# One decoder layer on one core: new addresses for the parts of the weights, and a new order of the products of a pair

## The chip, the cores and the metric

The kernel runs on one core of a Trainium2 chip. The metric is the time that the device takes for one execution, in microseconds (us); the table further down has the median of three runs. One further execution was taken with the hardware profiler, and all rows below are from it.

The engines go by short names: PE is the matmul engine (TensorE), PEld its loads of stationary operands, DVE the vector engine, ACT the scalar engine, POOL GpSimd, SP the queue that issues most transfers.

## The reference

One layer of a decoder, for 256 tokens and 16 learned meta tokens in front of them, width 2048, all in float32: half a SwiGLU feed-forward step of hidden width 5632 (FFN1), a mixer of two attentions, and a second half step (FFN2). Cut to what matters:

```python
h = h + 0.5 * swiglu(rmsnorm(h, ffn1_norm), ffn1_w_gate, ffn1_w_up, ffn1_w_down)
proj = rmsnorm(h, mix_norm) @ w_in      # q, k, v of 8 + 8 heads, 8 forget logits, two gates of 2048
o_fox = forgetting_attention(...)       # softmax with a decay from the forget gates
o_sb = stick_breaking_attention(...)
merged = sigmoid(g_fox) * (o_fox @ w_branch_fox) + sigmoid(g_sb) * (o_sb @ w_branch_sb)
h = h + merged @ w_out
h = h + 0.5 * swiglu(rmsnorm(h, ffn2_norm), ffn2_w_gate, ffn2_w_up, ffn2_w_down)
return h[:, 16:]
```

`swiglu(x, g, u, d)` is `(silu(x @ g) * (x @ u)) @ d`. Nearly all of the arithmetic is in products of an activation with a weight matrix.

## The kernel before

**Products in three terms.** The kernel multiplies float32 matrices in the faster type float32r, and wins the accuracy back by splitting: ACT copies a weight tile `raw` into `wh` in float32r, DVE writes the rest, `raw - wh`, into `wl` (function `split`, lines 163 to 165). Activations are split in the same way into a high and a low half. Of the four products of the halves three are made: high by high, high by low and low by high, all accumulated in one bank of PSUM.

**Blocks and units.** A `Block` is a column range of one weight matrix, 512 columns wide as a rule. It is worked in units of 1024 / columns k tiles (of 128 rows), so two k tiles: a *pair*. `load(u)` brings a unit of 512 KB into one of five `raw` buffers by one transfer on SP's queue, `split_unit(u)` makes `wh` and `wl` (three buffers each), and `products(u)` issues the matmuls. `ahead(u)` keeps loads six units ahead and splits two units ahead of the products. All units follow each other in one list through FFN1, the mixer and FFN2; the attention and the evacuations are dealt out between the output tiles by `tick()`.

**Which operand is stationary.** Each matmul on PE has a stationary operand of up to 128 x 128, loaded before it, and a moving operand that streams past it. There are these kinds of block:

- by feature, 272 columns (FFN1's blocks and the k and v blocks of both attentions): a 128-column slice of the weights is stationary, a half of an activation tile (256 tokens and 16 meta tokens) moves. Four output tiles a unit, six products each, 24 a unit;
- by token (the two gates, the two branches, FFN2): a 128-token slice of an activation half is stationary, a 512-column weight part moves. Two output tiles a unit, six products each, 12 a unit;
- wide (the q blocks and w_out): both activation halves move in one product of 512 columns by `wh`, and the high half in one of 256 by `wl`;
- the forget gate, `stacked`: one unit of eight k tiles of 128 columns, two products each.

**What sets the order.** The order on PE is that of the loop in `products` (line 930 on): for each output tile, for each of the two k tiles, the three terms. By feature they are `wh` by high, `wh` by low, `wl` by high (line 941). By token they are high by `wh`, high by `wl`, low by `wh` (line 934). In the first 25 us the ACT and DVE instructions stand in a hand-written order (`first_start`, `first_norm`, `first_products`), and the scheduler brings forward PE's products that are ready; there the first block's units wait for x, for the split and for the transposes.

**Addresses.** An activation tile is `[P, 2, 2, 272]` (k tile, half, tokens) in FFN1 and the mixer and `[P, 2, 2, 256]` in FFN2 and for the attentions' outputs, so its halves lie 1088 or 1024 bytes apart in each partition. A weight part is `[P, 2, 512]`: k tiles 2048 bytes apart, slices of 128 columns 512 bytes apart. The built program places the bases of all these tiles at equal remainders modulo 256.

## Time and profile before

| | |
|---|---|
| median of 3 runs | 2249.6 us (2248.21 to 2250.57) |
| the profiled execution | 2249.19 us, its span 2247.5 us |
| mean granted clock of PE | 0.999 |
| PE busy | 2240.8 us, 13930 matmuls |
| loads of stationary operands | 2039.6 us |
| DVE, ACT busy | 1265.4 us, 1024.6 us |
| transfers | 403 MB, 179 GB/s on average |
| FFN1 | up to about 817 us |
| mixer | up to about 1520 us |
| FFN2 | the rest |

A group of the page's fifth part, and of the view by lines, has the line, the engine, the operation, the tile written and the tiles read (an arrow between them), the shapes and the count; then the busy time, the mean of one instruction, the idle time of the engine just before them and what ended most of it. Matmuls overlap in their pipeline: one of 272 columns lasts 288 ns from its start to its end, while the next starts some 125 ns after it. So a duration is not what a product costs; the distance from start to start is. In names of tiles `v` is an activation, `acc` and `aux` are banks of PSUM.

### The profile page before, as it was taken

The page shows a single profiled execution, that of the slowest core. Times are in us where ns is not written, and L with a number is a line of the kernel's source. Part 1 is how long each engine was busy: PE and PEld are TensorE (multiplying, and loading weights), DVE is VectorE, ACT ScalarE, POOL GpSimd, SP SyncE. Part 2 cuts the span into 40 slices and gives each one's busy share as a digit, 9 for nine tenths or more (in the row PEclk, how much of TensorE's full clock was granted, in tenths as well). Part 3 has the DMA queues.
Part 4 walks back from the last instruction along what each step waited for, and adds up shares of the span by engine and source line. Part 5 has one row for each costly group of instructions (what it writes and reads, how often), then busy time and mean ns, then how long its engine had stood idle before and what let it go on. Part 6 is the DMA issues. An engine that isn't in the chain of part 4 may idle for free.

```text
span 2247.5 us, 34143 instructions
## 1 busy us (share of the span) xinstructions
PE 2240.8 (100%) x13930; PEld 2039.6 (91%) x13930; DVE 1265.4 (56%) x1596; ACT 1024.6 (46%) x1280; POOL 42.1 (2%) x112
## 2 busy tenths in 40 slices
PE   9999999999999999999999999999999999999999
PEld 9999999999999999988899988888888888888887
DVE  6555544455555555987556666675445544544554
ACT  6444433334444454655446564454444433444433
POOL 1000000000000001110000000000000000000000
PEclk9999999999999999999999999999999999999999
DMA  7666655566665566555655556566666666666664
GB/s 228 171 177 178 172 177 177 171 178 176 172 177 175 173 184 180 158 167 167 194 180 151 150 150 187 181 185 178 188 190 193 187 191 194 191 190 190 188 199 156
DMA packets 211325, 403.03 MB, mean 179 GB/s; under 512 B 12680, under 2 KB 17632, under 8 KB 211168
## 3 DMA queue, kind: packets, MB, share of 16 engines
q1 hardware_dynamic: 209088, 397.33, 59.1%
q8 instruction: 109, 1.79, 0.3%
q10 hardware_dynamic: 1472, 2.37, 0.3%
q0 software_dynamic: 608, 1.16, 0.2%
q14 instruction: 48, 0.39, 0.1%
HBM read 398.70 MB, written 2.11 MB: 178 GB/s over the span
## 4 chain that ended last, share of the span: by engine, by line
PE 99%; DMA 0%; SPq 0%; DVE 0%; issue 0%; DVEq 0%; ACT 0%
PE acc L944 96%; PE aux L701 1%; PE aux L572 1%; PE aux L412 1%; PE aux L672 0%; PE aux L560 0%; PE acc L914 0%; DMA v<-in_meta_tokens_dram 0%; PE aux L828 0%; PE aux L312 0%; PE aux L651 0%; PE aux L652 0%; PE aux L653 0%; PE aux L615 0%; PE aux L616 0%; PE aux L238 0%
## 5 line engine op out<-in xcount | busy, mean ns | idle before, releaser
L165 DVE TENSOR_TENSOR wl<-raw,wh 128x1024 fp32r<-128x1024 f32 (+1 forms) x753 | 921.4, 1224 | 857.3 <-ACT wh L164 855.8
L164 ACT ACTIVATE wh<-raw 128x1024 fp32r<-128x1024 f32 (+1 forms) x753 | 797.2, 1059 | 1096.2 <-PE acc L944 1029.7
L944 PE MATMUL acc<-v,wh 128*128 128x272 f32 (+1 forms) x5776 | 1172.9, 298 | 0.0
L944 PEld LDWEIGHTS acc<-v,wh 128*128 128x128 f32 x5776 | 923.6, 189 | 22.7
L944 PE MATMUL acc<-wh,v 128*128 128x512 f32 x2880 | 905.9, 391 | 0.0
L944 PE MATMUL acc<-v,wl 128*128 128x272 f32 (+1 forms) x3128 | 897.0, 287 | 0.0
L944 PEld LDWEIGHTS acc<-wh,v 128*128 128x128 f32 x2880 | 540.6, 188 | 111.7
L944 PEld LDWEIGHTS acc<-v,wl 128*128 128x128 f32 x3128 | 587.4, 188 | 0.4 <-DVE wl L165 0.2
L944 PE MATMUL acc<-wl,v 128*128 128x512 f32 x1440 | 561.3, 390 | 0.0
L944 PEld LDWEIGHTS acc<-wl,v 128*128 128x128 f32 x1440 | 270.5, 188 | 54.6
L164 ACT ACTIVATE v<-aux 128x512 fp32r<-128x512 f32 (+1 forms) x46 | 23.7, 516 | 19.2 <-PE aux L412 11.9
L165 DVE TENSOR_TENSOR v<-aux,v 128x512 fp32r<-128x512 f32 (+1 forms) x46 | 27.4, 595 | 4.3 <-ACT v L164 2.6
L440 DVE TENSOR_TENSOR sq<-acc,rbc 128x272 f32<-128x272 f32 x44 | 19.3, 438 | 18.5 <-PE acc L944 17.3
L431 DVE TENSOR_TENSOR v<-acc,rbc 128x272 f32<-128x272 f32 x44 | 18.0, 436 | 15.7 <-PE acc L944 15.7
L164 ACT ACTIVATE v<-sq 128x272 fp32r<-128x272 f32 x44 | 17.4, 419 | 19.5 <-DVE sq L441 19.5
L432 ACT ACTIVATE v<-v 128x272 f32<-128x272 f32 x44 | 17.5, 424 | 13.8 <-DVE v L431 13.8
L473 DVE SCALAR_TENSOR_TENSOR v<-acc,v 128x272 f32<-128x272 f32 x32 | 12.9, 435 | 12.6 <-PE acc L944 12.6
L441 DVE TENSOR_TENSOR sq<-sq,v 128x272 f32<-128x272 f32 x44 | 19.3, 438 | 0.8
L852 ACT ACTIVATE v<-acc,rtok 128x512 f32<-128x512 f32 x22 | 15.2, 690 | 9.9 <-PE acc L944 9.7
L412 PEld LDWEIGHTS aux<-ident,v 128*128 128x128 f32 x120 | 14.8, 140 | 3.7
L165 DVE TENSOR_TENSOR v<-sq,v 128x272 fp32r<-128x272 f32 x44 | 18.2, 434 | 0.0
L412 PE MATMUL aux<-ident,v 128*128 128x128 f32 x120 | 17.9, 272 | 0.0
(219 smaller groups left out, 725.7 us busy)
## 6 DMA issues: line engine op xcount, KB each, us to landing
raw<-in_ffn_w_up_dram SPq DMA_DIRECT2D x176, 512.0 KB, 3.7
raw<-in_ffn_w_down_dram SPq DMA_DIRECT2D x176, 512.0 KB, 3.9
raw<-in_ffn_w_gate_dram SPq DMA_DIRECT2D x175, 512.0 KB, 3.7
raw<-in_w_in_dram SPq DMA_DIRECT2D x162, 512.0 KB, 3.7
raw<-in_w_out_dram SPq DMA_DIRECT2D x32, 512.0 KB, 3.9
raw<-in_w_branch_fox_dram SPq DMA_DIRECT2D x16, 512.0 KB, 3.9
raw<-in_w_branch_sb_dram SPq DMA_DIRECT2D x16, 512.0 KB, 3.9
v<-in_x_dram SPq DMA_DIRECT2D x8, 256.0 KB, 7.8
```

The source lines that it names most:

```text
L164: act.activation(hi, src, AF.Copy)
L165: dve.tensor_tensor(lo, src, hi.bitcast(F32), op=ALU.subtract)
L412: pe.transpose(p[:, (2 * j + i) * P:(2 * j + i + 1) * P], u[:, i, c:c + P], ident[:])
L431: dve.tensor_tensor(s, ps[:, :n], norm_of().r[:, :n], op=ALU.mult)
L432: act.activation(s, s, AF.Silu)
L440: dve.tensor_tensor(u, ps[:, :n], norm_of().r[:, :n], op=ALU.mult)
L441: dve.tensor_tensor(u, u, s, op=ALU.mult)
L473: dve.scalar_tensor_tensor(r, ps[:, :NT], 0.5, r, op0=ALU.mult, op1=ALU.add)
L572: pe.matmul(po[:, :NR], a[:, ks], b[:, i * NR:(i + 1) * NR], start=n == 0, stop=n == 6)
L701: pe.matmul(o, a, b, start=start, stop=stop, skip_group_check=True)
L852: act.activation(u["t"][:, i, :], ps[:], AF.Silu, scale=norms["ffn2"].rtok[:, i:i + 1])
L944: pe.matmul(o, a, c, start=first and m == 0, stop=last and m == len(terms) - 1, skip_group_check=wide)
```

## The change

Four things change.

1. Each `wh` and `wl` tile becomes a flat one of 1088 columns, and a part is placed in it by kind of block (`place`, `part_tile`). By feature with 272 columns: the k tiles are 544 columns apart (2176 bytes, instead of 2048), and `wh` begins 16 columns (64 bytes) into its tile. For the gates, whose activations have 272 columns too (`spaced`): also 544 apart, `wh` begins 32 and `wl` 16 columns into the tile. For all other blocks parts stay dense and begin at the start.
2. The six products of a pair follow a table of (k tile, part of the weights: 0 high, 1 low, half of the activation: 0 high, 1 low): `FEATURE`, `TOKEN`, or `PLAIN` for the rest. The wide blocks and the forget gate keep their order. With these tables and places the next stationary operand lies, modulo 256, 64 bytes past the start of the moving one in the 272-column blocks, and 0 bytes past it in all blocks by token.
3. To make room in the memory of a partition (the two tags with three buffers each grow by 256 bytes a buffer), constants are merged: the identity and the ones are held once, in float32r, and read as float32 where needed; `gcol1` and `grow1` become slices of `gcol` and `grow`; one transfer of `ffn1_norm` is dropped. POOL writes the identity and the ones into a temporary tile, and DVE copies them at the start.
4. `first_products`, for the first unit, keeps its order, on the new addresses.

```diff
+PLAIN = ((0, 0, 0), (0, 0, 1), (0, 1, 0), (1, 0, 0), (1, 0, 1), (1, 1, 0))
+FEATURE = ((0, 1, 0), (0, 0, 0), (0, 0, 1), (1, 1, 0), (1, 0, 0), (1, 0, 1))
+TOKEN = ((0, 0, 1), (1, 1, 0), (1, 0, 1), (0, 0, 0), (1, 0, 0), (0, 1, 0))
+PART = 1024 + 64
...
+    plain = temp([P, 2, NT], F32, "F3")
+    make_identity(nc, plain[:, 0, :P])
+    nc.gpsimd.memset(plain[:, 1, :P], 1.0)
...
+    dve.tensor_copy(identr[:], plain[:, 0, :P])
+    dve.tensor_copy(onesr[:], plain[:, 1, :P])
...
+    def place(b):
+
+        if b.by_token:
+            return (TOKEN, (32, 16), 32) if b.spaced else (PLAIN, (0, 0), 0)
+        return (FEATURE, (16, 0), 32) if b.n == NT and not b.stacked else (PLAIN, (0, 0), 0)
+
+    def part_tile(u, low):
+        b, k0, n = units[u]
+        tag = ("wh", "wl")[low]
+        t = wp.tile([P, PART], F32R, tag=tag, name=name(tag))
+        order, at, free = place(b)
+        w = b.cols + free
+        return t[:, :n * w].rearrange("p (k c) -> p k c", k=n)[:, :, at[low]:at[low] + b.cols]
...
     def split_unit(u):
         b, k0, n = units[u]
-        wh = wp.tile([P, n, b.cols], F32R, tag="wh", name=name("wh"))
+        wh = part_tile(u, 0)
...
-                if b.by_token:
-                    xh, xl = x[:, 0, cs], x[:, 1, cs]
-                    terms = ((ps[:], xh, wh[:, i, :]), (ps[:], xh, wl[:, i, :]), (ps[:], xl, wh[:, i, :]))
...
+            elif b.by_token:
+                terms = [(ps[:], x[i][:, m, cs], w[l][:, i, :]) for i, l, m in place(b)[0]]
+            else:
+                terms = [(ps[:, :b.n], w[l][:, i, cs], x[i][:, m, :b.n]) for i, l, m in place(b)[0]]
+            for m, (o, a, c) in enumerate(terms):
+                pe.matmul(o, a, c, start=k0 == 0 and m == 0, stop=k0 + n == b.kts and m == len(terms) - 1,
+                          skip_group_check=wide)
```

How this moves the instructions on PE, at three places. The first is a unit in the middle of FFN1, before (a row is a line, the operation, the bank written, the tiles read, the shape; x2 stands for two equal ones in a row; the numbers behind the names tell tiles apart):

```order
L944 MATMUL acc_4246<-v_1907,wh_4306 128x272 x2
L944 MATMUL acc_4246<-v_1907,wl_4307 128x272
L944 MATMUL acc_4246<-v_1907,wh_4306 128x272 x2
L944 MATMUL acc_4246<-v_1907,wl_4307 128x272
L944 MATMUL acc_4247<-v_1907,wh_4306 128x272 x2
L944 MATMUL acc_4247<-v_1907,wl_4307 128x272
```

and a unit of the same kind after:

```order
L968 MATMUL acc_3874<-v_2964,wl_4085 128x272
L968 MATMUL acc_3874<-v_2964,wh_4084 128x272 x2
L968 MATMUL acc_3874<-v_2964,wl_4085 128x272
L968 MATMUL acc_3874<-v_2964,wh_4084 128x272 x2
L968 MATMUL acc_3875<-v_2964,wl_4085 128x272
L968 MATMUL acc_3875<-v_2964,wh_4084 128x272 x2
```

Of each three products of a k tile the one with `wl` stood third, and stands first now; the two with `wh` follow it, by the high and then the low half of the activation.

The second is the first output tile of a gate's unit, between products of the attention, before:

```order
L944 MATMUL acc_10779<-wh_10671,v_7861 128x512
L944 MATMUL acc_10779<-wl_10672,v_7861 128x512
L944 MATMUL acc_10779<-wh_10671,v_7861 128x512 x2
L944 MATMUL acc_10779<-wl_10672,v_7861 128x512
L944 MATMUL acc_10779<-wh_10671,v_7861 128x512
L615 MATMUL aux_10787<-kqh_10737,onesr 128x272
```

and after:

```order
L968 MATMUL acc_10775<-wh_10667,v_7857 128x512
L968 MATMUL acc_10775<-wl_10668,v_7857 128x512
L968 MATMUL acc_10775<-wh_10667,v_7857 128x512 x3
L968 MATMUL acc_10775<-wl_10668,v_7857 128x512
L627 MATMUL aux_10783<-kqh_10733,onesr 128x272
```

The three products with `wh` that stand next to each other belong to both k tiles now, and the six visit the k tiles in turn.

The third is the first unit of line 944 at the start (transposes of x ahead of it), before:

```order
L312 MATMUL aux_253<-ident,v_126 128x128 x2
L312 MATMUL aux_254<-ident,v_126 128x128 x2
L944 MATMUL acc_198<-v_220,wh_227 128x272 x2
L944 MATMUL acc_199<-v_220,wh_227 128x272 x2
L944 MATMUL acc_200<-v_220,wh_227 128x272 x2
L944 MATMUL acc_201<-v_220,wh_227 128x272 x2
L944 MATMUL acc_198<-v_220,wl_228 128x272
L944 MATMUL acc_198<-v_220,wh_227 128x272 x2
```

and after (line 968 is the same call as line 944 before, line 324 the transposes):

```order
L324 MATMUL aux_251<-identr,v_124 128x128 x2
L324 MATMUL aux_252<-identr,v_124 128x128 x2
L968 MATMUL acc_196<-v_218,wl_226 128x272
L968 MATMUL acc_196<-v_218,wh_225 128x272 x2
L968 MATMUL acc_196<-v_218,wl_226 128x272
L968 MATMUL acc_196<-v_218,wh_225 128x272 x2
L968 MATMUL acc_197<-v_218,wl_226 128x272
L968 MATMUL acc_197<-v_218,wh_225 128x272 x2
```

The scheduler had put all eight products with `wh` and the high or low half of the first k tile ahead of the first with `wl`; now a product with `wl` is the unit's first.

## Rows read from the trace of the kernel before

**Rows 1.** The page's header, its first part (busy time, share of the span and instructions of each engine) and PE's line of its second part (40 slices of the span).

```profile
span 2247.5 us, 34143 instructions
PE 2240.8 (100%) x13930; PEld 2039.6 (91%) x13930; DVE 1265.4 (56%) x1596; ACT 1024.6 (46%) x1280; POOL 42.1 (2%) x112
...
PE   9999999999999999999999999999999999999999
```

**Rows 2.** The page's fourth part: the chain that ended last, by engine.

```profile
PE 99%; DMA 0%; SPq 0%; DVE 0%; issue 0%; DVEq 0%; ACT 0%
```

**Rows 3.** The page's fifth part, groups of instructions (columns as told above): the splits, and the loads of `wl`.

```profile
L165 DVE TENSOR_TENSOR wl<-raw,wh 128x1024 fp32r<-128x1024 f32 (+1 forms) x753 | 921.4, 1224 | 857.3 <-ACT wh L164 855.8
L164 ACT ACTIVATE wh<-raw 128x1024 fp32r<-128x1024 f32 (+1 forms) x753 | 797.2, 1059 | 1096.2 <-PE acc L944 1029.7
...
L944 PEld LDWEIGHTS acc<-v,wl 128*128 128x128 f32 x3128 | 587.4, 188 | 0.4 <-DVE wl L165 0.2
```

**Rows 4.** The view by lines on PE over the whole span, shapes kept apart: line 944.

```profile
L944 PE MATMUL acc<-v,wh 128*128 128x272 f32 x5264 | 991.4, 288 | 0.0
L944 PE MATMUL acc<-wh,v 128*128 128x512 f32 x2880 | 905.9, 391 | 0.0
L944 PE MATMUL acc<-v,wl 128*128 128x272 f32 x2616 | 753.4, 289 | 0.0
L944 PE MATMUL acc<-wl,v 128*128 128x512 f32 x1440 | 561.3, 390 | 0.0
```

**Rows 5.** Windows (us from the span's start; the length, then the busy time and count of each engine, then PE's granted clock as a share of 2.4 GHz, the share of the DMA engines and GB/s): two at the start, and one of FFN1.

```profile
7.40:10.80 3.40, 3.08 (x15) 2.94 (x14) 3.23 (x9) 1.11 (x3) 0.76 (x4) 0.50 1.01 342
...
14.20:20.00 5.80, 5.80 (x47) 5.59 (x46) 5.18 (x14) 5.80 (x23) 0.00 (x0) 1.00 1.07 354
300.00:600.00 300.00, 300.00 (x2391) 300.00 (x2391) 149.23 (x176) 115.39 (x128) 0.00 (x0) 1.00 0.58 175
```

**Rows 6.** Line 944 in a stretch of FFN1, 300 to 400 us: the form and count, the shortest, median and longest duration in ns, the start of the first and the last in us.

```profile
L944 PE MATMUL acc<-v,wh x532: 285/288/292, 299.9 to 399.9; 128*128 128x272 f32 x178
L944 PE MATMUL acc<-v,wl x266: 287/288/290, 299.8 to 399.6; 128*128 128x272 f32 x133
```

**Rows 7.** The same view in a stretch of FFN2, 1800 to 1900 us.

```profile
L944 PE MATMUL acc<-wh,v x295: 389/389/389, 1799.9 to 1899.9; 128*128 128x512 f32 x148
L944 PE MATMUL acc<-wl,v x148: 389/389/389, 1799.7 to 1899.6; 128*128 128x512 f32 x148
```

**Rows 8.** The same view in two instants of FFN1 (400.42 and 400.79 us), so that only two or three products are in it: the two of `wh` on the first k tile, then the two of `wh` on the second, and the two of `wl`.

```profile
L944 PE MATMUL acc<-v,wh x2: 289/290/292, 400.1 to 400.3; 128*128 128x272 f32 x2
L944 PE MATMUL acc<-v,wl x1: 287/287/287, 400.4 to 400.4; 128*128 128x272 f32 x1
...
L944 PE MATMUL acc<-v,wh x2: 285/286/287, 400.5 to 400.6; 128*128 128x272 f32 x2
L944 PE MATMUL acc<-v,wl x1: 290/290/290, 400.8 to 400.8; 128*128 128x272 f32 x1
```

**Rows 9.** The same view in a gate's blocks, 1353.2 to 1356.6 us.

```profile
L944 PE MATMUL acc<-wh,v x10: 387/392/398, 1353.2 to 1356.2; 128*128 128x512 f32 x10
L944 PE MATMUL acc<-wl,v x6: 388/392/396, 1353.0 to 1356.4; 128*128 128x512 f32 x6
```

**Rows 10.** The timeline of PE in the same blocks (start in us, time until the last of the row ends, engine, line, operation, tiles, shape, count; equal ones that follow each other are one row).

```profile
1353.18 0.62 PE L944 MATMUL acc<-wh,v 128*128 128x512 f32 x2
...
1356.63 0.62 PE L944 MATMUL acc<-wh,v 128*128 128x512 f32 x2
```

**Rows 11.** The timeline of PE through one pair in FFN1, and the first row of the next output tile.

```profile
400.14 0.42 PE L944 MATMUL acc<-v,wh 128*128 128x272 f32 x2
400.39 0.29 PE L944 MATMUL acc<-v,wl 128*128 128x272 f32 x1
400.52 0.41 PE L944 MATMUL acc<-v,wh 128*128 128x272 f32 x2
400.76 0.29 PE L944 MATMUL acc<-v,wl 128*128 128x272 f32 x1
400.89 0.42 PE L944 MATMUL acc<-v,wh 128*128 128x272 f32 x2
```

**Rows 12.** The timeline of all engines at the start: DVE's first full `wl` splits, and PE's first products of three units.

```profile
13.13 1.23 DVE L165 TENSOR_TENSOR wl<-raw,wh 128x1024 fp32r<-128x1024 f32 x1 [0.46 <-ACT wh L164]
...
13.15 1.26 PE L944 MATMUL acc<-v,wh 128*128 128x272 f32 x8
...
14.41 0.39 PE L944 MATMUL acc<-v,wl 128*128 128x272 f32 x1
...
16.51 1.23 DVE L165 TENSOR_TENSOR wl<-raw,wh 128x1024 fp32r<-128x1024 f32 x1 [0.45 <-ACT wh L164]
...
16.88 1.24 PE L944 MATMUL acc<-v,wh 128*128 128x272 f32 x8
...
19.68 1.23 DVE L165 TENSOR_TENSOR wl<-raw,wh 128x1024 fp32r<-128x1024 f32 x1
...
20.32 0.87 PE L944 MATMUL acc<-v,wh 128*128 128x272 f32 x5
```

**Rows 13.** The view of waits on PE: what it waited for, us in total, times, the longest.

```profile
PE aux L303 <- DMA v<-in_meta_tokens_dram: 1.4, 2, 0.8
```

More of the change, by code (lines that the diff above doesn't have):

```diff
@@ L96, in drain @@
             tick()
-    ident = const([P, P], F32, "ident")
-    make_identity(nc, ident)
-    ones = const([P, P], F32, "ones")
-    nc.gpsimd.memset(ones[:], 1.0)
+    identr = const([P, P], F32R, "identr")
+    ident = identr[:].bitcast(F32)
+    onesr = const([P, P], F32R, "onesr")
+    ones = onesr[:].bitcast(F32)
+    plain = temp([P, 2, NT], F32, "F3")
+    make_identity(nc, plain[:, 0, :P])
+    nc.gpsimd.memset(plain[:, 1, :P], 1.0)
     eps_c = const([P, 1], F32, "eps")
@@ L249, in by_feature @@
             n, ps = self.n, aux()
-            pe.matmul(ps[:, :n], ones[:], self.acc[:, :n], start=True, stop=True)
+            pe.matmul(ps[:, :n], ones, self.acc[:, :n], start=True, stop=True)
             y = temp([P, NT], F32, "sq", bufs=2)[:, :n]
@@ L394, in first_factors @@
         p = aux()
-        pe.matmul(p[:, :NR], ones[:], diag[:, :NR], start=True, stop=True)
+        pe.matmul(p[:, :NR], ones, diag[:, :NR], start=True, stop=True)
         pe.matmul(p[:, NR:NT], ones[:NM, :], diag[:NM, NR:NT], start=True, stop=True)
@@ L802, in hybrid_layer @@
     for c in range(4):
-        blocks.append(Block(wi, 0, KT, 6152 + c * 512, 512, mrhs, NR, gate_evac("f", c), True))
+        blocks.append(Block(wi, 0, KT, 6152 + c * 512, 512, mrhs, NR, gate_evac("f", c), True, spaced=True))
     for c in range(4):
@@ L811, in hybrid_layer @@
     for c in range(4):
-        blocks.append(Block(wi, 0, KT, 8200 + c * 512, 512, mrhs, NR, gate_evac("s", c), True))
+        blocks.append(Block(wi, 0, KT, 8200 + c * 512, 512, mrhs, NR, gate_evac("s", c), True, spaced=True))
     for c in range(4):
@@ L894, in split_unit @@
             return
-        wl = wp.tile([P, n, b.cols], F32R, tag="wl", name=name("wl"))
-        split(wh[:], wl[:], raws.pop(u)[:])
+        wl = part_tile(u, 1)
+        split(wh, wl, raws.pop(u)[:])
         halves[u] = (wh, wl)
@@ L901, in split_half @@
         if i == 0:
-            halves[u] = tuple(wp.tile([P, n, b.cols], F32R, tag=t, name=name(t)) for t in ("wh", "wl"))
+            halves[u] = tuple(part_tile(u, low) for low in range(2))
         wh, wl = halves[u]
@@ L928, in products @@
             cs = slice(j * P, (j + 1) * P)
-            for i in range(n):
-                x = b.rhs(k0 + i)
-                first, last = k0 + i == 0, k0 + i == b.kts - 1
-                if b.by_token:
-                    xh, xl = x[:, 0, cs], x[:, 1, cs]
-                    terms = ((ps[:], xh, wh[:, i, :]), (ps[:], xh, wl[:, i, :]), (ps[:], xl, wh[:, i, :]))
-                elif wide:
-                    terms = ((ps[:].rearrange("p (a t) -> p a t", a=2), wh[:, i, cs], x[:, :, :NR]),
-                             (ps[:, :NR], wl[:, i, cs], x[:, 0, :NR]))
-                elif b.stacked:
-                    terms = tuple((ps[:, :b.n], wh[:, i, cs], x[:, m, :b.n]) for m in range(2))
-                else:
-                    o, xh, xl = ps[:, :b.n], x[:, 0, :b.n], x[:, 1, :b.n]
-                    terms = ((o, wh[:, i, cs], xh), (o, wh[:, i, cs], xl), (o, wl[:, i, cs], xh))
-                for m, (o, a, c) in enumerate(terms):
-                    pe.matmul(o, a, c, start=first and m == 0, stop=last and m == len(terms) - 1,
-                              skip_group_check=wide)
+            x = [b.rhs(k0 + i) for i in range(n)]
+            w = wh, wl
+            if wide:
+                terms = [t for i in range(n)
+                         for t in ((ps[:].rearrange("p (a t) -> p a t", a=2), wh[:, i, cs], x[i][:, :, :NR]),
+                                   (ps[:, :NR], wl[:, i, cs], x[i][:, 0, :NR]))]
+            elif b.stacked:
+                terms = [(ps[:, :b.n], wh[:, i, cs], x[i][:, m, :b.n]) for i in range(n) for m in range(2)]
+            elif b.by_token:
[5 more added lines that the diff above has]
+                          skip_group_check=wide)
             if wide and k0 + n == b.kts:
```

45 lines of the change are left out of this document (21 added, 24 removed).

## The prediction

> **What bounds the kernel now.** I read the page's header first: TensorE (PE) is busy for 2240.8 of 2247.5 us [rows 1], and past the first 11 us its granted clock is 1.00 wherever I looked [rows 5]. The chain that ended last says the same: 99% PE, 96% of it line 944 [rows 2], the matmul of `products`. Hardly anything waits in front of it: in the page's group of loads of `wl` the idle time is 0.4 us, 0.2 of it for DVE [rows 3], and ACT's split sits idle for PE, not the other way round. So the time is a number of matmuls times the distance between their starts, and the change can act on that distance alone.
>
> How many: line 944 by form has 5264 + 2616 = 7880 products of 272 columns and 2880 + 1440 = 4320 of 512 columns with a weight tile moving [rows 4]. (The wide blocks come on top.)
>
> How far apart: in a clean stretch of FFN1, 798 products of 272 columns start between 299.8 and 399.9 us [rows 6], so 100.1 / 797 = 125.6 ns each. At the full 2.4 GHz, 272 columns take 113.3 ns, so 12.2 ns per product is not columns. In FFN2, 443 products of 512 columns start between 1799.7 and 1899.9 [rows 7]: 226.7 ns against 213.3, that is 13.4 ns over.
>
> **What the address has to do with it.** The rows that decided me are the duration spreads. In FFN2 every one of 443 products takes 389 ns, shortest and longest alike [rows 7]. In FFN1 the same form spreads over 285 to 292 ns [rows 6], and the spread is not noise: the six products of a pair repeat one pattern. In the pair at 400.14 us the two of `wh` on the first k tile take 292 and 289, `wl` 287, the two on the second k tile 285 and 287, `wl` 290 [rows 8]. In the gates the spread is 387 to 398 [rows 9]. What differs by position is the address: halves of an activation tile lie 272 x 4 = 1088 bytes apart, which is 64 more than a multiple of 256, while weight parts and their 128-column slices lie at multiples of 512. With the bases equal modulo 256, the stationary operand of the next product, which is loaded while this one streams, lies by the code 0, 192, 0, 128, 64, 128 bytes past the start of the moving one in FFN1's six. In FFN2 the activation slices, now the stationary operands, come from tiles of 256 columns, and all distances are 0. Constant distance, constant duration; mixed distances, a spread.
>
> From the starts that the trace holds for line 944, in ns where the timeline's rows show tens of ns, I took the time from each product of 272 columns to the next and grouped it by that distance modulo 256 (7,845 intervals, out of the 7880 products of rows 4): 0 gives 127.2, 64 gives 122.6, 128 gives 125.0, 192 gives 127.6. Modulo 512 the groups don't split further. The timeline agrees as far as its rounding goes: from the `wh` pair of the first k tile, at distances 0 and 192, to the next product it is 0.25 us, from that of the second, at 128 and 64, 0.24, and the whole pair of six takes 0.75 [rows 11]. For 512 columns the gates run 230.0 each (15 products from 1353.18 to 1356.63 [rows 10]) and FFN2 226.7.
>
> **The change, part by part.**
>
> (a) The 272-column products in the new order. Of the 7880, 16 are the forget gate's block, whose order and addresses stay; 7864 remain, and each now has its next stationary operand 64 bytes past. If each takes what the 64-byte ones take now: 7864 x (125.6 - 122.6) = -23.6 us. No row shows a run of products that all have 64, so this is a value carried over from single products, and I bound it. Below: no overhead at all, 113.3 ns, -96.7 us. Above: the longest product of the pattern is 292 against a mean of (292 + 289 + 287 + 285 + 287 + 290) / 6 = 288.3; if all were that slow, +3.7 x 7864 = +29 us. I take 122.6, the row nearest to what the change makes.
>
> (b) The gates: 8 blocks x 8 units x 12 = 768 products go from mixed distances to 0, which is FFN2's case: 768 x (230.0 - 226.7) = -2.5 us. This is shown by a stage that has it already.
>
> (c) The other 512-column products (FFN2, branches: 3552) change only the order of the three terms. Distance 0 before and after; in FFN2 the three terms have one duration [rows 7]. Nothing. The wide blocks keep order and distances modulo 256. Nothing.
>
> (d) `wl` first. In the new order the first product of a unit reads `wl`, which DVE writes last. In steady state that is 250 ns earlier than before, and the splits run two units of 3.0 us ahead. At the start they don't: in the first three units of line 944 the old order runs eight, eight and five products of `wh` while DVE still writes `wl` [rows 12]. The first unit would start with `wl` at 14.41 instead of 13.15, 1.26 us later. Behind the waiting product stand 23 more and the transposes that feed ACT. The second unit's `wl` (DVE from 16.51, ready at 17.74) and the third's (from 19.68) pace the rest: unit 1 ends near 17.4 instead of 16.5, unit 2 starts at 17.9 and ends at 20.9, with transposes the third starts at about 21.3 and ends at 24.3 instead of 23.5. ACT, busy for all 5.80 us from 14.2 to 20 [rows 5], paces the same stretch. Some +0.9 us; from +0.3, if ACT alone sets the pace, to +2.6, if the wait costs another stretch of 3.4 us at granted clock 0.50, as the one from 7.4 to 10.8 is [rows 5].
>
> (e) The constants: two casts on DVE at the start, before the first transposes; a POOL DMA goes. PE waits there for meta tokens (1.4 us [rows 13]), which hides 0.3 us of casts. Temporary tiles move by up to 1.6 KB, which can shift the attention's some 300 products by a few ns each: about 1 us either way, taken as nothing. ACT and DVE write their splits in two pieces of 512 instead of one of 1024; at 1059 and 1224 ns per 3.0 us unit they have room [rows 3].
>
> Sum: -23.6 - 2.5 + 0.9 = -25.2 us. The profiled execution took 2249.2 us (span 2247.5 plus 1.7 around it), 0.4 under the median of the runs: 2249.2 - 25.2 = 2224.
>
> The Trainium skill, "TensorE: Matmul & The Clock Gate", section "Wait — 56ns, not 53.3ns?", has back-to-back products at their columns plus about 2.5 ns. The rows show 12.2 and 13.4 over [rows 6, 7]. By the page 9.7 ns of a 272-column product would be there to win, an estimate of 76 us over 7864 of them, and no row reaches it.
>
> **The rivals.**
>
> *One step each.* The overheads look like multiples of one step: 13.4 ns at distance 0 is two of 6.67; the six products of FFN1 together have 73.3, which is eleven. Then five of the six pay two steps and one pays one, and the one with the lowest interval is the one at 64 bytes; the uneven ns between are only where the start of the next one is put. If every product pays one step, it takes 120.0: 7864 x 5.6 = -44.0, total -45.6: 2204. For it: the sums come out whole. Against it: no single interval group is below 122.6.
>
> *Reading by durations.* The 64-byte product itself lasts 287, only 1.3 under the mean of 288.3; what its start-to-start gains, the neighbour's (290) gives back. Then 7864 x 1.3 = -10.2, total -11.8: 2237. The rows carry this as well as the 122.6; it goes halfway to the next.
>
> *The distance does nothing by itself.* The six intervals sum to the same whatever one calls each, and the cause could be the accumulator or the order. Then only (d) is left: 2250. FFN2's one duration speaks against it. The Trainium skill, "SBUF — State Buffer", section "SBUF: two separate sides", speaks for it: PE has a second, independent read port for the stationary operand, so addresses should not meet at all. By that rule the spread of durations has no cause; the trace disagrees with it as far as the spread goes [rows 6].
>
> *A constant distance is a constant stall.* Where the distance is already constant, in FFN2, each product pays 13.4; where it is mixed, at 272 columns, 12.2, because some escape. FFN2's activations end where they began modulo 256, those of 272 columns 64 bytes further: 64 past the start is then exactly FFN2's 0 past the end. If that is what counts, each product pays 13.4 and takes 126.7: 7864 x 1.1 = +8.7, with -2.5 and +0.9: 2256. It decides as soon as the mean in FFN1 rises above 126.4. For it: the one constant case in the trace. Against it: the gates, at 512 columns, are better constant than mixed.
>
> **How the numbers follow.** Forecast, 122.6 each: 0.36, own range 2216 to 2232. One step each: 0.22. Durations: 0.08. Nothing: 0.12. Constant stall: 0.22. This kernel's measurement tells 0.2%, 4.5 us, from no change: faster is the first three, 0.66; same 0.12; slower 0.22. The range for 8 in 10 goes from the one-step case, 2202, to the constant stall, 2257; that it holds cases of both signs is the unknown of (a), which no row shows in steady state.
>
> **What would show it.** By the products of 272 columns that start in 300 to 400 us: 816 for the forecast, 833 for one step, 798 for nothing, 789 for the stall; a spread of durations that closes to two or three values in either of the extreme cases. In the gates, 15 products in 3.40 us. At the start, the first product of line 944's successor behind DVE's first full `wl`. FFN2 at 389 ns as before. I am wrong if FFN1's spread stays 285 to 292 with the new order, or if its mean is above 125.6.

## The result, and the profile after

The changed kernel takes 2258.1 us in the median of 6 runs (2257.7 to 2259.6), the kernel before 2249.8 (2248.2 to 2250.6): a ratio of 1.004, with a 95% interval of 1.0028 to 1.0052. It is 8 us slower, where I had forecast 25 us faster, and 1 us above the range.

The page's header after, its first part and PE's line of its 40 slices, as in [rows 1]:

```profile
span 2256.4 us, 34143 instructions
PE 2248.0 (100%) x13930; PEld 2047.5 (91%) x13930; DVE 1268.8 (56%) x1596; ACT 1025.1 (45%) x1280; POOL 41.1 (2%) x111
...
PE   9999999999999999999999999999999999999999
```

As many PE instructions as before, PE as full as before, and a span 8.9 us longer (2256.4 against 2247.5). So each product takes longer to make way for the next. The stretch of FFN1 that the prediction named, 300 to 400 us (line 968 is the old 944; columns as in [rows 6]):

```profile
L968 PE MATMUL acc<-v,wh x528: 288/289/291, 299.7 to 399.8; 128*128 128x272 f32 x176
L968 PE MATMUL acc<-v,wl x264: 286/289/293, 300.0 to 399.9; 128*128 128x272 f32 x132
```

528 + 264 = 792 products start there, where 798 did: (399.9 - 299.7) / 791 = 126.7 ns each against 125.6. The prediction had 816 for its forecast and 789 for the constant stall. And the spread, 286 to 293 ns, is as wide as the 285 to 292 of before, although every product now has the same distance. The timeline shows the six that repeat:

```profile
400.04 0.42 PE L968 MATMUL acc<-v,wh 128*128 128x272 f32 x2
400.30 0.29 PE L968 MATMUL acc<-v,wl 128*128 128x272 f32 x1
400.42 0.41 PE L968 MATMUL acc<-v,wh 128*128 128x272 f32 x2
400.67 0.29 PE L968 MATMUL acc<-v,wl 128*128 128x272 f32 x1
400.80 0.42 PE L968 MATMUL acc<-v,wh 128*128 128x272 f32 x2
```

From 400.04 to 400.80 a round of six takes 0.76 us, before it took 0.75 [rows 11]. In ns the starts in the trace are 123, 124, 128, 131, 129, 125 apart: 760 for the six, twelve steps of 6.67 ns over the columns' 680, where before there were eleven (753).

The gates, with the stretch of [rows 10], do gain:

```profile
1354.41 0.39 PE L968 MATMUL acc<-wl,v 128*128 128x512 f32 x1
...
1355.78 0.39 PE L968 MATMUL acc<-wl,v 128*128 128x512 f32 x1
```

Six products in 1.37 us are 228.3 ns each; over the two gates' 384 products each, wherever one follows directly on another, the starts are 231.6 and 230.2 ns apart, against 233.0 and 231.1 before: 384 x (1.4 + 0.9) = 0.9 us gained. FFN2 shows 389 ns for each of its 443 products in 1800 to 1900 us, as in [rows 7]. At the start, the view of waits on PE (us in all, times, the longest), to be read beside [rows 13]:

```profile
PE acc L968 <- DVE wl L175: 2.0, 2, 1.3
```

The timeline shows the two, and DVE's first `wl` (compare [rows 12]):

```profile
12.32 1.23 DVE L175 TENSOR_TENSOR wl<-raw,wh 128x1024 fp32r<-128x1024 f32 x1 [0.48 <-ACT wh L174]
...
13.60 0.39 PE L968 MATMUL acc<-v,wl 128*128 128x272 f32 x1 [1.33 <-DVE wl L175]
...
36.11 0.39 PE L968 MATMUL acc<-v,wl 128*128 128x272 f32 x1 [0.70 <-DVE wl L175]
```

The order that begins with `wl` waits twice for DVE, 2.0 us in all; before, nothing of `products` waited so long [rows 3]. Start by start, the same product comes 1.2 us later at 41 us, 7.6 at 772, 8.9 at 978 and 8.9 in FFN2. So the loss in this pair of executions is 1.2 us at the start and then a steady 1.1 ns for each 272-column product. The 1.2 is a difference of two executions whose transfers landed at different times: DVE's first full `wl` began at 13.13 us before and at 12.32 after, so that counted from it the same product is 2.0 us later.

### The profile page after: what moved, and what is told of

Read it like the earlier page. It is cut to its first block, busy times and chain, and to the rows that moved or that the text cites. A ratio compares the mean times of both kernels' runs of the same rounds, so it can differ in the third digit from the quotient of the medians.

```text
span 2256.4 us, 34143 instructions
## 1 busy us (share of the span) xinstructions
PE 2248.0 (100%) x13930; PEld 2047.5 (91%) x13930; DVE 1268.8 (56%) x1596; ACT 1025.1 (45%) x1280; POOL 41.1 (2%) x111
## 4 chain that ended last, share of the span: by engine, by line
PE 99%; DVE 0%; DMA 0%; ACT 0%; issue 0%; SPq 0%; DVEq 0%; ACTq 0%
PE acc L968 96%; PE aux L713 1%; PE aux L584 1%; PE aux L424 1%; PE aux L572 0%; PE aux L684 0%; DMA v<-in_meta_tokens_dram 0%; DVE wl L175 0%; PE aux L840 0%; PE acc L940 0%; PE aux L664 0%; PE aux L627 0%; PE aux L663 0%; PE aux L324 0%; PE aux L665 0%
## 5 line engine op out<-in xcount | busy, mean ns | idle before, releaser
L968 PE MATMUL acc<-wh,v 128*128 128x512 f32 x2880 | 893.1, 391 | 0.0
L424 PEld LDWEIGHTS aux<-identr,v 128*128 128x128 f32 x120 | 14.9, 140 | 3.7
L186 DVE TENSOR_TENSOR R<-F,R 128x512 fp32r<-128x512 f32 x16 | 11.0, 690 | 12.5 <-ACT R L185 12.4
L424 PE MATMUL aux<-identr,v 128*128 128x128 f32 x120 | 18.0, 272 | 0.0
```

The source lines that it names most:

```text
L186: dve.tensor_tensor(lo[:, :n], src[:, :n], hi[:, :n].bitcast(F32), op=ALU.subtract)
L424: pe.transpose(p[:, (2 * j + i) * P:(2 * j + i + 1) * P], u[:, i, c:c + P], ident)
L968: pe.matmul(o, a, c, start=k0 == 0 and m == 0, stop=k0 + n == b.kts and m == len(terms) - 1, skip_group_check=wide)
```

## Which of the two, order or address?

My theory by now: the price of a product is not set by its own distance, but by the whole walk of both operands (the addresses that they take from product to product), round after round. The rivals: each product pays for its distance and 64 is dear in a long run; the walk of the moving operand (x) alone sets the price; the loss has nothing to do with addresses. Three kernels take the change apart, and a fourth program runs walks alone. In all kernels below, constants and tiles are as in the changed one.

**Order alone.** New order, dense old addresses:

```diff
-            return (TOKEN, (32, 16), 32) if b.spaced else (PLAIN, (0, 0), 0)
-        return (FEATURE, (16, 0), 32) if b.n == NT and not b.stacked else (PLAIN, (0, 0), 0)
+            return (TOKEN if b.spaced else PLAIN, (0, 0), 0)
+        return (FEATURE if b.n == NT and not b.stacked else PLAIN, (0, 0), 0)
```

> The new order of the products with the old, dense addresses of the weight parts; all else as in the changed kernel. Distances then are 0, 0, 64, 128, 128, 192 in each six, the same mixture as in the kernel before. If each product pays by its own distance: 125.6 ns per 272-column product as before, about 2250 us. If the walk of the moving operand sets the price: 126.7 ns, 2257 to 2259 us, as the changed kernel. If the pattern of both operands sets it, neither of these two times.

Measured: 2252.9 us, ratio 1.0016 (1.0007 to 1.0024). In FFN1, 300 to 400 us:

```profile
L968 PE MATMUL acc<-v,wh x532: 286/288/291, 299.9 to 399.8; 128*128 128x272 f32 x178
L968 PE MATMUL acc<-v,wl x267: 287/287/288, 299.7 to 399.9; 128*128 128x272 f32 x134
```

799 products: 125.6 ns, as before, to a hundredth over all of FFN1 (125.55 and 125.56). So the walk of x alone is out. But the 125.6 ns is the price that I had expected of the rule of own distances, and not of my theory, which said neither; the next run has to decide between these two. The 3.6 us are elsewhere: the gates' starts are 235.0 and 233.9 ns apart, 384 x (2.0 + 2.8) = 1.8 us over before, and `wl` is waited for 2.0 us as in the changed kernel.

**Addresses alone.** Old order, new addresses:

```diff
-            return (TOKEN, (32, 16), 32) if b.spaced else (PLAIN, (0, 0), 0)
-        return (FEATURE, (16, 0), 32) if b.n == NT and not b.stacked else (PLAIN, (0, 0), 0)
+            return (PLAIN, (32, 16), 32) if b.spaced else (PLAIN, (0, 0), 0)
+        return (PLAIN, (16, 0), 32) if b.n == NT and not b.stacked else (PLAIN, (0, 0), 0)
```

> The new addresses of the weight parts with the old order of the products; all else as in the changed kernel. Distances then are 64 and twice 192 in each three. If each product pays by its own distance, by the single intervals of the kernel before (122.6 + 2 x 127.6) / 3 = 125.9 ns, 2250 to 2253 us. If the walk of the moving operand sets the price: 125.6 as before, 2248 to 2251 us. If the pattern of both operands sets it, neither, and 120 to 127 ns, 2206 to 2261 us, are open.

Measured: 2266.5 us, ratio 1.0081 (1.0068 to 1.0095). The same view:

```profile
L968 PE MATMUL acc<-v,wh x523: 290/297/298, 299.8 to 399.9; 128*128 128x272 f32 x175
L968 PE MATMUL acc<-v,wl x261: 286/286/286, 300.0 to 399.6; 128*128 128x272 f32 x131
```

784 products: 127.8 ns, thirteen steps a round, and outside all that I had expected, the 120 to 127 of my theory too. By its own distances this kernel should have paid 125.9; it pays more than the dearest single interval of the kernel before (127.6). In 300 to 400 us the two products at distance 64 take 126.0 ns each here, where 64 had 122.4 in the same stretch before, and the four at 192 take 135.0 and 122.4 in turn. So the rule of own distances is out as well.

**The gates alone.** Everything of the 272-column products as before:

```diff
-        return (FEATURE, (16, 0), 32) if b.n == NT and not b.stacked else (PLAIN, (0, 0), 0)
+        return (PLAIN, (0, 0), 0)
```

> Order and addresses as before for the 272-column products, new order and new addresses in the two gates' blocks alone; constants and tiles as in the changed kernel. If the 272-column products are the whole loss, 2247 to 2250 us; the gates' 768 products at 229.1 instead of 230.0 ns give 0.7 us. If the moved constants or the larger tiles cost something of their own, 2251 or more.

Measured: 2248.8 us, ratio 0.9998 (0.9989 to 1.0007). The 272-column products are back at 125.6 ns, so they are the loss (with the wait for `wl`, which comes with their order), and constants and larger tiles cost nothing that shows. Against this kernel, order alone is 4.1 us slower: 2.7 from the gates (384 x (3.4 + 3.7) ns), and 1.4 are left for `wl` first.

So for 272 columns the two halves of the change do not add up: order alone 0, addresses alone +2.2 ns, both together +1.1. In the gates each half alone loses (235.0 and 234.1 ns in the first gate, against 233.0) and both together win (231.6).

**Walks alone.** Nothing but products on PE, 96 of each walk, one PSUM tile per walk; the walks are addresses only:

```python
mv = [Q * (s * i % 4) for i in range(MANY)]
st = [0] + [(mv[i] + Q * d) % 64 for i in range(MANY - 1)]
...
pe.matmul(ps[:, :n], sta[:, st[k]:st[k] + P], mov[:, mv[k]:mv[k] + n],
          start=k == 0, stop=k == MANY - 1)
```

> Leaves the whole computation out (x is copied to the output): 80 walks of 96 products each, one PSUM tile per walk, nothing else beside them on TensorE. A walk's name gives the columns (r 272, q 256, w 512), then by how many bytes the next stationary operand lies past the start of the moving one (a 0, b 64, c 128, d 192), then the step of the moving operand from product to product (a 0, b 64, c 128, d 192). If the distance alone sets the price, walks with the same second letter have one interval, whatever the third: by the single intervals of the kernel before 127.2, 122.6, 125.0 and 127.6 ns for ra, rb, rc, rd. If the step of the moving operand sets it, walks with the same third letter have one interval, whatever the second, and the four second letters agree within 1 ns. If both matter, rows and columns of the table both differ. The walk named old (the six products of a pair before) should give 125.6 and new 126.7 by any theory that looks at addresses alone; if they agree within 0.3 ns, addresses of the operands are not the cause.

The timeline (start, time until the last of the row ends, tile, count); the time of a walk is the next row's start less its own, over 96:

```profile
57.47 12.00 PE L61 MATMUL ps_rba<-mov,sta 128*128 128x272 f32 x96
69.31 12.24 PE L61 MATMUL ps_rbb<-mov,sta 128*128 128x272 f32 x96
81.39 12.02 PE L61 MATMUL ps_rbc<-mov,sta 128*128 128x272 f32 x96
93.25 12.16 PE L61 MATMUL ps_rbd<-mov,sta 128*128 128x272 f32 x96
105.25 12.32 PE L61 MATMUL ps_rca<-mov,sta 128*128 128x272 f32 x96
...
471.47 22.56 PE L61 MATMUL ps_wba<-mov,sta 128*128 128x512 f32 x96
493.87 22.09 PE L61 MATMUL ps_wbb<-mov,sta 128*128 128x512 f32 x96
515.80 22.24 PE L61 MATMUL ps_wbc<-mov,sta 128*128 128x512 f32 x96
...
1090.80 12.21 PE L61 MATMUL ps_old<-mov,sta 128*128 128x272 f32 x96
1102.85 12.32 PE L61 MATMUL ps_new<-mov,sta 128*128 128x272 f32 x96
1115.00 12.41 PE L61 MATMUL ps_oldnew<-mov,sta 128*128 128x272 f32 x96
1127.25 12.26 PE L61 MATMUL ps_newold<-mov,sta 128*128 128x272 f32 x96
```

The four walks that all have distance 64 (rba to rbd) take 11.84, 12.08, 11.86 and 12.00 us: 123.3, 125.8, 123.5 and 125.0 ns, where the distance rule wants one number. At 512 columns the same distance gives 233.3 in one walk and 228.4 in the next (wba, wbb). The old six take 12.05 us, 125.5 ns, the new six 12.15, 126.6, the new addresses in the old order 12.25, 127.6: three of the four kernels' prices within 0.2 ns, from addresses alone, with no weights streaming in, no DVE, no ACT. That settles the last rival, that addresses have nothing to do with it. The fourth, order alone, took 126.1 here and 125.6 in the kernel; the next section has to do with that. The Trainium skill, "SBUF — State Buffer", section "Who interferes with whom", gives PE two independent read ports, one for each operand, and has contention only where GpSimd and DVE share one; these runs disagree, by up to 4.5 ns of 126, since PE works alone in them and the walks differ in their operands' addresses.

## What a walk costs, and whether it keeps its price

**224 more walks**, 221 of them drawn at random: the six products of a pair in any order, the four weight parts at any multiple of 64 bytes, 60 products each. A walk's name has the order (0 to 5 are the six products as they stood before), then where `wh` and `wl` of the first k tile and `wh` and `wl` of the second begin, in units of 64 bytes in this program and the next, of 16 bytes in later ones.

> Leaves the whole computation out (x is copied to the output): 231 walks of 60 products of 272 columns, back to back. Each walk repeats the six products of a pair in an order of its own (the digits), with the four weight parts wh0 wl0 wh1 wl1 at addresses of their own (in 64 bytes modulo 256), the parts of x 0, 64, 128, 192 as in the kernel. Three more have both operands of the old walk moved by the same 64, 128, 192 bytes. If the walk of both operands sets the price, the walks 012345_0000, 201534_1032, 012345_1032, 201534_0000 give again 125.4, 126.7, 127.7 and 126.1 ns within 0.3, the three moved walks 125.4, and the 224 drawn at random spread from about 123.3 (one and a half steps of 6.67 ns, the least of the 272-column walks in the first such run) to 128; at least one below 124.0. If each product pays by its own distance, the walks with the same mixture of distances agree, and the least is that with the most distances of 64. If addresses don't matter, all agree within 0.5 ns.

Measured, from the starts of each walk's 6th to 54th product: 123.3 to 127.8 ns, in the mean 125.4. The old walk, moved as a whole by 64, 128 or 192 bytes, takes 125.1 to 125.5; where it stood first in the program it held PE's own start and isn't counted. I compared each walk with the mean of its six single intervals, 127.2, 122.6, 125.0 and 127.6 by distance: over 227 walks the correlation is 0.02. The 18 walks with the very mixture of distances of the kernel before take 124.4 to 126.9. The distance rule is dead, and not because a number was off.

**512 columns.**

> Leaves the whole computation out (x is copied to the output): walks of 60 products with the weights moving, 512 columns. f: the stationary parts of x all at one address modulo 256, as in FFN2. g: at 0, 64, 128, 192, as in the gates. Order and the weight parts' addresses drawn at random, 80 each; h and q: constant addresses, the stationary one 0 to 240 bytes past the moving one in steps of 16, 512 and 256 columns. f012345_0000 should give FFN2's 226.7 ns, g012345_0000 the gates' 230.0 of the kernel before, g154032_2103 the 229.1 of the changed kernel. If two steps (226.7) are the least that a 512-column product can pay, no walk falls below it; if 1.5 steps can be had here too, the best fall to 223.3.

The FFN2 walk that stood first held PE's start; its like in the new order took 226.7. No walk falls below that, so FFN2 already has the least that the other 175 walks of this width show, and most walks cost it 230 to 234. FFN2's two steps are what a lucky walk pays there, not what any constant distance pays: with the stationary operand 64 bytes past, all constant, it is 233.3. The new gates' walk alone took 227.8, where I had expected 229.1, and the old gates' walk 234.4, not 230.0: a miss, the second one by far.

**The same walk from different starts.**

> Leaves the whole computation out (x is copied to the output): walks of 60 products again. The first 30 are five walks (before, changed, new addresses in the old order, walk a, and one more), each begun at each of its six products: if a walk has one price, the six agree within 0.1 ns; if the price depends on the state in which a walk starts, they differ by whole fractions of 6.67 ns a cycle. q and r: constant addresses, 256 and 272 columns, the stationary operand 0, 64, 128 or 192 bytes past the moving one (first digit), only the very first stationary operand elsewhere (second digit): by one price the second digit changes nothing. The rest are drawn at random, with the weight parts in steps of 16 bytes (x), and with the high parts of x next to each other (y): if 123.3 ns is the least that 272 columns can have, none falls below it; 120.0, one step, if not.

The second digit does change something. The timeline, with walks q and r in turn; the first pair is distance 64 with the first stationary operand at 0, the second pair the same with it at 192:

```profile
1527.33 7.23 PE L83 MATMUL ps_q<-mov,sta 128*128 128x256 f32 x60
1534.40 7.57 PE L83 MATMUL ps_r<-mov,sta 128*128 128x272 f32 x60
...
1703.07 6.98 PE L83 MATMUL ps_q<-mov,sta 128*128 128x256 f32 x60
1709.88 7.57 PE L83 MATMUL ps_r<-mov,sta 128*128 128x272 f32 x60
```

One product of 60 lies elsewhere, and 256 columns take 7.07 us in the first case, 117.8 ns each, and 6.81 in the second, 113.5: one and two thirds steps over the columns against one, kept to the end. Whether this one product did it or what ran ahead of the walk, the pair can't tell: with all 60 at distance 64, the very same addresses took 117.8 ns each in this program and 113.3 in the program of 512-column walks, where another walk ran ahead of them (ps_q here, ps_qe there):

```profile
1585.87 7.23 PE L83 MATMUL ps_q<-mov,sta 128*128 128x256 f32 x60
...
2328.98 6.97 PE L75 MATMUL ps_qe<-mov,sta 128*128 128x256 f32 x60
```

272 columns at a constant distance (r) take one time whatever the first product was. Of the walks of six, the changed kernel's takes 126.6 to 126.9 from four starts and 125.6 from two. Walk a, the best of the draw at 123.3, takes 125.0 from five of its six starts and 126.7 from one; the first of the six is the very walk of the draw, product for product, and takes 125.0 now. So a walk can have more than one steady state, and what went before picks it. Of the 170 new walks drawn at random in this program none fell below the 123.3 of the first draw.

## Putting walks into the kernel

Four kernels have other walks for the 272-column products, with the changed kernel's gates. Walk a, the best of the draw, and walk b, 123.9 in it, were chosen before the starts were known. This is walk a:

```diff
-FEATURE = ((0, 1, 0), (0, 0, 0), (0, 0, 1), (1, 1, 0), (1, 0, 0), (1, 0, 1))
+FEATURE = ((0, 0, 0), (0, 0, 1), (1, 0, 0), (0, 1, 0), (1, 0, 1), (1, 1, 0))
...
-        return (FEATURE, (16, 0), 32) if b.n == NT and not b.stacked else (PLAIN, (0, 0), 0)
+        return (FEATURE, ((0, 16, -1), (0, 32, 1))) if b.n == NT and not b.stacked else (PLAIN, ((0, 0, 1), (0, 0, 1)))
...
-        return t[:, :n * w].rearrange("p (k c) -> p k c", k=n)[:, :, at[low]:at[low] + b.cols]
+        return t[:, :n * w].rearrange("p (k c) -> p k c", k=n)[:, ::turn, at:at + b.cols]
```

(each part now has its own start, free columns, and a turn that lays the second k tile first; walk b has the order 043125 and other numbers)

> The changed kernel with another walk for the 272-column products, the best of the 224 drawn at random: order 013245, parts wh0 wl0 wh1 wl1 at 64, 0, 0, 128 bytes modulo 256. It took 123.33 ns a product when it ran alone, and its distances are 64, 192, 128, 0, 192, 192. If the walk of both operands sets the price and the kernel falls into the same cycle: 7864 x (125.6 - 123.3) = 18 us less than before, and the gates' 0.7: 2229 to 2234 us. If each product pays by its own distance, by the single intervals of the kernel before (122.6 + 3 x 127.6 + 125.0 + 127.2) / 6 = 126.3 ns, 2252 to 2256 us. If the cycle depends on what went before it, anything between 2231 and 2250.

> As the run before it, with the walk 043125 and the parts at 192, 64, 64, 0 bytes, which took 123.9 ns a product alone: 7864 x 1.7 = 13 us less than before and the gates' 0.7, 2234 to 2239 us if the walk sets the price; if the cycle depends on what went before it, up to 2250.

Walk a: 2244.6 us in the median, ratio 0.9989 (0.9978 to 1.0): some 5 us less than before in the median, and not the 18 that were hoped for. Two of its eleven runs took 2254.3 and 2255.9 us, the other nine 2244.0 to 2246.3, at a mean granted clock of 0.999 to 1.00 in all. Walk b: 2235.4, ratio 0.9939 (0.9925 to 0.9953), as expected. Line 968 in 300 to 400 us, with walk a:

```profile
L968 PE MATMUL acc<-v,wh x534: 283/287/292, 299.9 to 399.9; 128*128 128x272 f32 x178
L968 PE MATMUL acc<-v,wl x268: 287/288/290, 299.8 to 399.8; 128*128 128x272 f32 x134
```

The same view with walk b:

```profile
L968 PE MATMUL acc<-v,wh x539: 282/287/291, 299.8 to 399.9; 128*128 128x272 f32 x180
L968 PE MATMUL acc<-v,wl x270: 287/288/288, 300.1 to 399.8; 128*128 128x272 f32 x135
```

802 and 809 products. Walk a settles at 125.0 ns in FFN1, just what it takes from most starts alone, and not at the 123.3 that the draw had seen. Its other price turns up in the profiled execution too: in the mixer, from 845 to 882 us, the starts are 126.7 ns apart with the same walk, and later 125.0 again. In 850 to 880 us, 239 products:

```profile
L968 PE MATMUL acc<-v,wh x159: 287/288/297, 849.9 to 879.8; 128*128 128x272 f32 x159
L968 PE MATMUL acc<-v,wl x80: 288/288/289, 849.8 to 879.9; 128*128 128x272 f32 x80
```

At 126.7 throughout, the kernel would take 7864 x 1.7 = 13 us more; that the two runs some 10 us above the others fell into this price for most of their time is likely, but neither was profiled, and it is not shown. So the next program took 37 walks and began each at each of its six products:

> Leaves the whole computation out (x is copied to the output): 37 walks of 272-column products, each begun at each of its six products, 60 products a start. Walk b (043125_c440), the walk before (012345_0000), the changed one (201534_40c8), walk a (013245_4008), and the 33 best of the two searches. If a kernel's price for a walk is the one most starts settle to, walk b gives 123.9 in at least four of six starts (the kernel with it ran at 123.9), walk a 125.0 to 125.3, the walk before 125.1 to 125.6, the changed one 126.6 to 126.9. If walk b's six are as scattered as walk a's, what a kernel falls into can't be told from walks alone. A walk with all six starts at or below 123.6 would be one to put into the kernel.

Measured, walk b from five starts 123.9 to 124.2 (the sixth was the program's first walk, which held PE's own start); the walk before 125.1 to 125.6; the changed one 125.6 to 126.9; walk a 125.0 to 125.1 and once 126.7. Over all 37 walks it was 123.3 to 128.3. From two walks with all six starts close together I made the last kernels. Walk c has order 021453; walk d keeps the old order and moves addresses alone:

```diff
-FEATURE = ((0, 1, 0), (0, 0, 0), (0, 0, 1), (1, 1, 0), (1, 0, 0), (1, 0, 1))
+FEATURE = ((0, 0, 0), (0, 0, 1), (0, 1, 0), (1, 0, 0), (1, 0, 1), (1, 1, 0))
...
-        return (FEATURE, (16, 0), 32) if b.n == NT and not b.stacked else (PLAIN, (0, 0), 0)
+        return (FEATURE, ((48, 0, 0, 1), (16, 16, 16, -1))) if b.n == NT and not b.stacked else (PLAIN, ((0, 0, 0, 1),) * 2)
```

> The changed kernel with the walk 021453_2d15 for the 272-column products (parts wh0 wl0 wh1 wl1 at 32, 208, 16, 80 bytes modulo 256), whose six starts alone took 123.3 to 124.1 ns, 123.7 in the mean. If the kernel's price is the one that the starts settle to: 7864 x (125.5 - 123.7) = 14.5 us less than before and the gates' 0.7, 2232 to 2237 us. If addresses that are no multiples of 64 bytes cost something of their own when the parts are written or loaded, more than 2237.

> The order of the kernel before, and only the parts' addresses changed for the 272-column products: walk 012345_ccc8 (192, 192, 192, 128 bytes modulo 256), whose six starts alone took 124.3 to 124.8, 124.5 in the mean; the gates as in the changed kernel. If the kernel's price is the one that the starts settle to: 7864 x 1.0 = 8 us less than before and the gates' 0.7, 2238 to 2243 us. If the order has to change for a gain, 2248 to 2250.

Walk c: 2234.7 us, ratio 0.9936 (0.9922 to 0.9949). Walk d: 2239.9, ratio 0.9961 (0.9949 to 0.9974). Both inside what was expected, and faster than either kernel of this case, if by less than 1%. The same view with walk c:

```profile
L968 PE MATMUL acc<-v,wh x542: 283/284/288, 299.8 to 399.9; 128*128 128x272 f32 x181
L968 PE MATMUL acc<-v,wl x271: 285/286/286, 299.9 to 399.8; 128*128 128x272 f32 x136
```

And with walk d:

```profile
L968 PE MATMUL acc<-v,wh x537: 287/288/288, 299.7 to 399.8; 128*128 128x272 f32 x179
L968 PE MATMUL acc<-v,wl x269: 286/286/288, 299.9 to 399.9; 128*128 128x272 f32 x135
```

All eight side by side (ns per 272-column product; alone, over the starts that were run, and in the kernel from the starts in 100 to 830 us):

| kernel | alone | in FFN1 | us |
|---|---|---|---|
| before | 125.1 to 125.6 | 125.55 | 2248.8 to 2249.8 |
| changed | 126.6 to 126.9, twice 125.6 | 126.67 | 2258.1 |
| order alone | 126.1 (one start) | 125.56 | 2252.9 |
| addresses alone | 127.7 to 127.8, once 123.3 | 127.78 | 2266.5 |
| walk a | 125.0 to 125.1, once 126.7; in the draw 123.3 | 125.00 | 2244.6 |
| walk b | 123.9 to 124.2 | 123.89 | 2235.4 |
| walk c | 123.3 to 124.1 | 123.33 | 2234.7 |
| walk d | 124.3 to 124.8 | 124.44 | 2239.9 |

Durations tell nothing here: walk d's are the closest together (286 to 288 ns) and it isn't the fastest; walk b's lie 282 to 291 apart and it beats walk d by 4.5 us.

## Why the prediction was wrong

*What bounds the kernel* was right: PE, product after product, with the address deciding how far apart they start. The same work on other addresses and in other orders runs anywhere from 2234.7 to 2266.5 us.

*Term (a)* failed: "if each takes what the 64-byte ones take now", 122.6 ns, -23.6 us. Measured 126.67 in FFN1, so 7864 x 1.1 = +8.7. (The forget gate's block has 32 products under the line, in two units, and not 16, so 7848 change; that moves no sum by 0.1 us.) Two readings went into the term. The first was that a group's interval is the price of its members. It is one part of a round whose sum alone is a price: in a round of six the start of each product ends one interval and begins the next, so what one gains the next can lose. The sums were whole numbers of steps in the kernel before, the changed one and the one with addresses alone (eleven, twelve, thirteen), and 10.5 and 9.5 with walks a and b. The prediction's own rivals said that neighbours give and take, under "one step each" and "reading by durations", and the forecast still took the group's mean. The trace before could have told: in 300 to 400 us the two products of a round at distance 0 take 128.3 and 125.0 ns, the two at 128 take 123.3 and 126.7, so that one distance had two prices already, and the means by distance hid it. The second was that a constant distance gives a constant duration. FFN2 was the only stage with one distance, and it was constant in everything else too; the changed FFN1 has one distance and durations from 286 to 293.

*Term (b)*, -2.5 for the gates: the sign was right, the size was off; 0.9 us. They didn't fall to FFN2's 226.7: the new gates' walk takes 227.8 alone, and none of the 80 walks drawn with x's parts stepping by 64 bytes, as in the gates, came below that, while three of those with x's parts at one address, as in FFN2, did.

*Term (c)*, nothing: right; FFN2 stays at 389 ns, and the changed kernel is 8.9 us late at 1408 us and 8.9 at the end.

*Term (d)*, +0.9 with +0.3 to +2.6: the waits came, 1.33 and 0.70 us. Their price is 1.2 us by the starts at 41 us in one pair of executions, 2.0 counted from DVE's first full `wl` in the same pair, and 1.4 by what is left between the medians of two kernels with 11 runs each; the last is the best of the three. But the second wait was not where I put it, in units two and three, but at 36 us, where DVE comes late from other work: the small instructions of the norm and two parts of the activations keep it until 34.85, the split until 36.06.

*Term (e)*, nothing: right by the kernel with the gates alone.

*The rivals.* "A constant distance is a constant stall" gave 126.7 and 2256, and that is the price that came. Its mechanism is not what the runs show: the durations are not constant, and the same distance costs 123.3 or 125.8 in another walk. I can't count it as right. "The distance does nothing by itself" is what the 227 walks say, but the time it gave, 2250, assumed that then nothing else of the addresses matters.

The sum as measured: +8.7 for the 272-column products, -0.9 for the gates, +1.2 at the start, 9.0; the runs' medians differ by 8.3, the two profiled spans by 8.9.

*Open:* what inside the chip makes a step. The runs show that the price belongs to the walk of both operands and to the state in which it starts. The six products of a round together cost whole or half steps of 6.67 ns in the kernels here; a step is 16 columns at 2.4 GHz (the granted clock is 1.00 there), or 64 bytes of a row. No rule that I tried gives the price of a walk without running it. Why order alone takes 125.6 in the kernel and 126.1 alone may lie in the start, but it was run from one start only. That the bases of the kernel's tiles are equal modulo 256 is known from the built program; no trace shows it.

## What to carry to other kernels

A mean over a group of products that alternate with others is not a price that can be multiplied: sum over the whole repeating round, and change the round as a whole. Where PE is full, try a few dozen address patterns of the inner round in a small program, each from several starts, and take into the kernel one whose starts agree; walks b, c and d ran in the kernel's FFN1 within 0.4 ns of the mean of their starts, while walk a's 123.3, seen in one program alone, came neither in the kernel nor in the next two programs. Three walks are few, and agreement is no warrant: walk c too has a stretch of the mixer, from 1125 to 1165 us, at 125.6 ns and not 123.3. Where an order begins with the part that is ready last, look for its waits wherever the splitting engine is late, not at the beginning alone.

## What I had not expected of the hardware

Products of one shape, 272 columns of float32r with a new stationary operand each, run back to back in 123.3 to 128.3 ns by addresses alone and what went before, 512 columns in 226.7 to 234.4, 256 columns in 113.3 to 120.1. The least are 6.7 ns over the columns at 256 (113.3 against 106.7), 10.0 at 272 and 13.3 at 512. The Trainium skill, "TensorE: Matmul & The Clock Gate", section "Wait — 56ns, not 53.3ns?", has about 2.5 ns over the columns for back-to-back products; no walk of these runs comes nearer than 6.7, at 256 columns. And the same 60 products at the same addresses can take 117.8 ns each in one program and 113.3 in another, for as long as they were watched.
